# Start addresses of the standing weights, and 21 transposes whose result nobody reads

## The chip, the cores and the metric

The kernel runs on one core of a Trainium2 chip. The metric is the device time of one execution in microseconds (us); it is taken over several executions, and the median counts. A profile is one further execution, recorded instruction by instruction, with a time of its own.

## The reference

The reference is one layer of a decoder trunk for 256 tokens (SEQ) of width 2048 (D_MODEL), everything in float32:

```
h = rms_norm(x, norm1_g);  proj = h @ w_in              # 2048 x 6152: q, k, v of 8 + 8 heads, 8 gate columns
y_a = fox_attention(...);  y_b = dilated_attention(...)
x = x + concat(rms_norm(y_a, g_a), rms_norm(y_b, g_b)) @ w_out      # 2048 x 2048
h = rms_norm(x, norm2_g)
x = x + square(relu(h @ w_mlp_in)) @ w_mlp_out          # 2048 x 8192 and 8192 x 2048
return rms_norm(x, final_norm_g)
```

Nearly all the work lies in the four weight matrices, some 201 MB together, each of which is read once.

## The kernel before

**Three products for one.** A float32 product is made of three products in the fp32r type: a number is split into an upper part (what is left after it is rounded to fp32r) and a lower part (the rest), and upper x upper, upper x lower and lower x upper are summed in PSUM. The activations are split once and lie in `aT_hi`, `aT_lo` (input of a layer, features on the partitions) and in `yT_hi`, `yT_lo` (shown as `big_hi`, `big_lo` in the profile). The weights arrive in float32 in `raw` and are split as they come: ScalarE writes the upper part (`whi`, L180), VectorE the lower part (`wlo`, L181). One split covers 256 rows of a weight matrix by 512 columns; four buffers of `whi` and four of `wlo` are in turn.

**Chunks.** The program is a list of chunks of 512 weight columns. For each chunk 16 row blocks of 128 are multiplied (8 for half of w_out). There are two forms, and they matter here:

- *Weights moving* (chunks v, o and d: values, output projection, MLP down). The activations are loaded into the TensorE array as the standing operand, 128 columns wide, and 512 weight columns stream past (L314 to L316). A product is a load of 128 columns (PEld in the profile) and a MATMUL of 512 columns.
- *Weights standing* (chunks q, k and u, named in `TURNED`: queries, keys, MLP up). 128 weight columns are loaded, and the 256 tokens stream past (L331). The result comes out turned, features on the partitions, as the next stage wants it. For each of the four blocks of 128 weight columns three products follow each other: upper weights by `aT_hi`, the same upper weights by `aT_lo`, lower weights by `aT_hi`. There are 1536 of each of the three, 4608 in all: 1536 in the eight chunks q and k, in the first 310 us, and 3072 in the sixteen chunks u, in four stretches of 768 that alternate with the chunks d.

**Addresses.** All of this is about where in a partition an operand begins. A float32 element has 4 bytes. `whi` and `wlo` are tiles of 2*512 + 64 elements, 4352 bytes, which is 17 x 256 bytes; in the built program the first lies at byte 125952 = 492 x 256, so that all eight begin at a multiple of 256. A view into the tile skips the first `b` elements (L162 to L166):

```
            b = FAR if chunks[ci][0] in TURNED else NEAR
```

With `NEAR` = 8 a part begins 32 bytes behind a multiple of 256, with `FAR` = 56 it begins 224 bytes behind one. A block of 128 weight columns is 512 bytes, so all blocks begin at the same remainder. `aT_hi`, `aT_lo`, `big_hi` and `big_lo` lie 32 bytes behind a multiple of 256 (a small tile named `ahead`, L246, shifts them), and their rows of 256 tokens are 1024 bytes. So in the form "weights moving" both operands begin at 32, and in the form "weights standing" the moving operand begins at 32 and the load at 224.

**Transposes without a reader.** `settle` (L354) takes a PSUM tile and transposes the identity matrix into it three times. Nothing reads the tile. It runs at the end of each chunk v and at the end of each stretch of chunks d but the last: seven times, 21 transposes. Each of these places is where a stretch of weights moving ends and one of weights standing begins. There is one more such place, at the first chunk u, and there no `settle` stands.

**What sets the order.** The order is written out by hand. The main loop (L776 to L786) runs over the steps (256 weight rows each), issues the splits three steps ahead, and then the products of the step; side work (norms, attention, draining an accumulator) is hung on a product's number with `at` and is issued behind it by `run_side`. TensorE runs its instructions in this order; between two products of a chunk stand, now and then, the transposes and small products of the side work.

Of the kernel before, what the change touches and what calls it, by code (L numbers as in the profile page):

```python
# [11 lines left out]
F32 = mybir.dt.float32  # L12
# [7 lines left out]
P = 128  # L20
# [18 lines left out]
LEAD = 3  # L39


LINE, NEAR, FAR = 64, 8, 56
TURNED = "qku"
WARM, WARM2 = 8, 1

# [27 lines left out]
def kernel(  # L73
# [18 lines left out]
    nc = tc.nc  # L92
# [12 lines left out]
    psum = ctx.enter_context(tc.tile_pool(name="psum", bufs=2, space=PSUM))  # L105
# [4 lines left out]
    chunks = []  # L110
# [41 lines left out]
    def split(i, j0=0, n=2):  # L152
        if i >= len(steps):
            return
        if j0:
            return split_rows(i, j0, n)
        ci, s = steps[i]
        t = raws[ci, s // 2][:, 2 * (s % 2):2 * (s % 2) + 2, :]
        if ci == len(chunks) - 1 and s < 4:
            hi, lo = (a[:, 4 * s:4 * s + 4, :].rearrange("p (k j) s -> p k (j s)", k=2) for a in (aT_hi, aT_lo))  # L160
        else:
            b = FAR if chunks[ci][0] in TURNED else NEAR  # L162
            hi, lo = (
                wsplit.tile([P, 2 * CW + LINE], F32R, name=n)[:, b:b + 2 * CW].rearrange("p (j c) -> p j c", j=2)
                for n in ("whi", "wlo")
            )  # L166
        if chunks[ci][5] > CW:
            f = wsplit.tile([P, 2, 2 * NH], F32R, name="wf")
            fh, fl = f[:, :, :NH], f[:, :, NH:]
            nc.gpsimd.tensor_copy(fh, t[:, :, CW:])  # L170
            nc.gpsimd.tensor_tensor(fl, t[:, :, CW:], fh.bitcast(F32), op=ALU.subtract)
            forget_w[i] = f
        splits[i] = (hi, lo)
        split_rows(i, j0, n)

    def split_rows(i, j, n):
        ci, s = steps[i]
        hi, lo = (a[:, j:j + n, :] for a in splits[i])
        t = raws[ci, s // 2][:, 2 * (s % 2) + j:2 * (s % 2) + j + n, :CW]
        nc.scalar.activation(hi, t, AF.Copy)  # L180
        nc.vector.tensor_tensor(lo, t, hi.bitcast(F32), op=ALU.subtract)  # L181
# [4 lines left out]
    ident = one.tile([P, P], F32, name="ident")  # L186
# [148 lines left out]
    def products(i, j):  # L335
# [13 lines left out]
        if cols > CW:  # L349
            for n, part in enumerate(a[:2]):  # L350
                nc.tensor.matmul(accs["f"][:2 * NH, :SEQ], forget_w[i][:, j], part[:, kt, :],  # L351
                                 start=go and n == 0, stop=end and n == 1)

    def settle():  # L354

        p = psum.tile([P, 512], F32, name="tr")
        for n in range(3):
            nc.tensor.transpose(p[:, n * P:(n + 1) * P], ident, ident)  # L358


    side = {}
# [1 line left out]
    def at(i, f, *a):  # L363
        side.setdefault(i, []).append((f, a))
# [140 lines left out]
    probs, turned = {}, {}  # L505
# [171 lines left out]
    def last_chunk(done):  # L677

        ci = len(chunks) - 1
        what, key, _, _, _, _, kts = chunks[ci]  # L680
        i0 = len(steps) - kts // 2
        c0 = D_MODEL - CW
        for t, a, b, n in ((0, 0, CW, 3), (1, 0, CW // 2, 3), (1, CW // 2, CW, 4)):
            acc = psum.tile([P, CW], F32, name="acc", bufs=4)
            for kt in range(kts):
                if t == 0 and kt % 2 == 0:
                    split(done + 1 + kt // 2)
                product(acc[:, :b - a], operands(what, key), kt, t, splits[i0 + kt // 2], kt % 2, slice(a, b),
                        kt == 0, kt == kts - 1)
                if t == 0:  # L690
                    run_side(2 * i0 + kt)
            if b == CW:
                sum_before(t, n)
            add_down(acc, t, slice(c0 + a, c0 + b), n)
            if b == CW:
                finish(t, n, slice(c0 + a, c0 + b))
# [6 lines left out]
    for ci, (what, key, *_rest) in enumerate(chunks[:-1]):  # L703
        e = last_slot[what, key]
        if what == "v":
            at(e, drain_v, key, ci)
            at(e, settle)
            if key == 0:
                at(e, drain_f)
                at(e + 2, forget_gates)  # L710
                at(e + 6, gate_sums)
                at(e + 4, rel_row)
                at(e + 5, rel_back)
                at(e + 55, rel_turn)
        elif what in "qk":
            for half in range(2):
                late = half if what == "k" else (2 if key else 5) + 5 * half
                at(e + late, drain_qk, key, what, ci, half)
            if what == "k":
                kind = groups[key][4]  # L720
                for h in range(4):
                    n = e + 6 + 7 * (h // 2)
                    if kind == 0:
                        at(n - 3, decay_of, groups[key][3] * 4 + h)
                    at(n, scores, key, h)
                for h in range(4):
                    at(e + 20 + 7 * (h // 2), values, key, h)
                for h in range(4):
                    at(e + 13 + 7 * (h // 2), turn_probs, key, h)
                if key % 2:  # L730
                    at(e + 29, group_norm, kind)
        elif what == "o":
            at(e, drain_o, *key, ci)
            if key[0] == 1:
                at(e + 2, to_features, 4 * key[1], 16)
                at(e + 3, to_features, 4 * key[1] + 2, 16)
                if key[1] == 3:
                    at(e + 4, second_norm)
        elif what == "u":
            at(e, drain_u, key[1], ci)  # L740
        else:
            at(e, drain_d, *key, ci)
            if key[1] == 3:
                at(e, settle)
            if key == (ROUNDS - 1, 0):
                at(e - 8, load_gf)

    idle_products(WARM)
    split(0, 0, 1)
    gains(0, 16)  # L750
    to_features(0, 0, 1)
    split(0, 1, 1)
    to_features(1, 0, 1)
    idle_products(WARM2)
# [62 lines left out]
```

## Time and profile before

| | us |
|---|---|
| median of 3 timed executions | 1125.04 (1124.77 to 1125.28) |
| the profiled execution | 1123.52 |
| its span, from the first to the last instruction | 1121.7 |
| TensorE busy with products (PE) in the span | 1110.5 |
| TensorE busy with loads of the standing operand (PEld) | 1014.0 |
| VectorE, ScalarE, GpSimd busy | 643.0, 517.0, 33.3 |
| granted TensorE clock, mean | 0.998 |

The profile's page has a row for each group of instructions: its line, engine and operation, out<-in by the names of the tiles, the shapes, xcount, then the busy time in us and the mean time of one in ns, then the idle time of the engine before them. Products overlap in time: a MATMUL's own duration (280 ns) is longer than the distance to the next one. So what a product costs is read from the distance between starts, or from the length of a stretch divided by the number of products in it (the view of stretches, whose rows are: stretch from:to, its length, busy time of the engines and in brackets the number of instructions, granted clock, DMA share, GB/s).

### The profile page before, as it was taken

What the parts mean: (1) busy time and instruction counts of PE and PEld (TensorE: products, weight loads), DVE (VectorE), ACT (ScalarE), POOL (GpSimd) and SP (SyncE); (2) the same over time, 40 slices, a digit from 0 to 9 for tenths busy, and PEclk for the clock granted to TensorE, in tenths of its full rate; (3) what the DMA queues carried; (4) which work ended last, traced back from release to release, by engine and by line L of the source; (5) the groups of instructions that cost most, each with busy time, mean ns of one, the idle gap of its engine ahead of it and who ended that gap; (6) DMA issues with size and microseconds to landing.
All of it is one profiled execution on the core that took longest, in us unless ns stands there. A gap on an engine that the chain in (4) does not pass through costs nothing.

```text
span 1121.7 us, 17508 instructions
## 1 busy us (share of the span) xinstructions
PE 1110.5 (99%) x7362; PEld 1014.0 (90%) x7362; DVE 643.0 (57%) x805; ACT 517.0 (46%) x669; POOL 33.3 (3%) x58
## 2 busy tenths in 40 slices
PE   9999999999999999999999999999999999999996
PEld 7899899999988899998889998889998889999886
DVE  6666756656476675565545555555555554555564
ACT  6445545445454554553434454344444433454451
POOL 1100200000001000000000000000000000000000
PEclk9999999999999999999999999999999999999999
DMA  8665454545554556556565655565655566646641
GB/s 314 226 200 176 150 188 151 176 163 167 177 182 153 185 158 219 188 184 206 199 199 180 197 188 196 197 196 162 199 195 196 198 190 188 188 152 225 225 150 75
DMA packets 105098, 209.16 MB, mean 186 GB/s; under 512 B 3683, under 2 KB 4796, under 8 KB 104892
## 3 DMA queue, kind: packets, MB, share of 16 engines
q1 hardware_dynamic: 103868, 205.94, 55.4%
q0 software_dynamic: 304, 1.06, 0.4%
q8 instruction: 57, 0.93, 0.3%
q10 hardware_dynamic: 848, 1.06, 0.3%
q14 instruction: 21, 0.17, 0.0%
HBM read 205.93 MB, written 2.11 MB: 185 GB/s over the span
## 4 chain that ended last, share of the span: by engine, by line
PE 99%; DMA 0%; DVE 0%; POOL 0%; ACT 0%; DVEq 0%; issue 0%; ACTq 0%
PE acc L331 48%; PE acc L314 16%; PE acc L315 16%; PE acc L316 16%; PE sc L521 1%; PE sc L566 1%; PE tr L267 1%; PE tr L548 0%; DMA xs<-in_x_dram 0%; PE sc L351 0%; PE tr L358 0%; PE sc L518 0%; DVE xs L674 0%; PE sc L440 0%; PE tr L583 0%; POOL rstd L664 0%
## 5 line engine op out<-in xcount | busy, mean ns | idle before, releaser
L181 DVE TENSOR_TENSOR wlo<-raw,whi 128x1024 fp32r<-128x1024 f32 (+1 forms) x382 | 463.5, 1223 | 363.5 <-ACT whi L180 361.2
L180 ACT ACTIVATE whi<-raw 128x1024 fp32r<-128x1024 f32 (+1 forms) x382 | 399.5, 1053 | 406.9 <-PE acc L331 198.3
L331 PE MATMUL acc<-aT_hi,whi 128*128 128x256 f32 x1536 | 430.2, 280 | 0.1
L331 PE MATMUL acc<-aT_lo,whi 128*128 128x256 f32 x1536 | 427.0, 278 | 0.1
L331 PE MATMUL acc<-aT_hi,wlo 128*128 128x256 f32 x1536 | 426.6, 278 | 0.0
L331 PEld LDWEIGHTS acc<-aT_hi,whi 128*128 128x128 f32 x1536 | 288.3, 188 | 1.2 <-issue 0.6
L331 PEld LDWEIGHTS acc<-aT_hi,wlo 128*128 128x128 f32 x1536 | 288.3, 188 | 0.0
L331 PEld LDWEIGHTS acc<-aT_lo,whi 128*128 128x128 f32 x1536 | 287.9, 187 | 0.4 <-DVE aT_lo L257 0.3
L314 PE MATMUL acc<-whi,big_hi 128*128 128x512 f32 (+1 forms) x632 | 245.1, 388 | 0.0
L316 PE MATMUL acc<-wlo,big_hi 128*128 128x512 f32 (+1 forms) x632 | 244.4, 387 | 0.0
L315 PE MATMUL acc<-whi,big_lo 128*128 128x512 f32 (+1 forms) x632 | 244.3, 386 | 0.0
L316 PEld LDWEIGHTS acc<-wlo,big_hi 128*128 128x128 f32 x632 | 118.7, 188 | 24.2
L314 PEld LDWEIGHTS acc<-whi,big_hi 128*128 128x128 f32 x632 | 118.7, 188 | 23.7
L315 PEld LDWEIGHTS acc<-whi,big_lo 128*128 128x128 f32 x632 | 118.7, 188 | 23.4
L314 PE MATMUL acc<-whi,aT_hi 128*128 128x512 f32 x128 | 50.8, 397 | 0.0
L316 PE MATMUL acc<-wlo,aT_hi 128*128 128x512 f32 x128 | 50.1, 391 | 0.0
L315 PE MATMUL acc<-whi,aT_lo 128*128 128x512 f32 x128 | 50.0, 391 | 0.0
L254 DVE TENSOR_TENSOR big_lo<-nat,big_hi 128x512 fp32r<-128x512 f32 x32 | 22.2, 693 | 22.4 <-ACT big_hi L253 22.4
L253 ACT ACTIVATE big_hi<-nat 128x512 fp32r<-128x512 f32 x32 | 20.3, 634 | 26.1 <-DVE nat L615 26.1
L638 DVE SCALAR_TENSOR_TENSOR xs<-acc,rstd2sq,xs 128x512 f32<-128x512 f32 (+1 forms) x33 | 23.4, 734 | 10.6 <-PE acc L316 10.6
L316 PEld LDWEIGHTS acc<-wlo,aT_hi 128*128 128x128 f32 x128 | 24.0, 188 | 5.3
L314 PEld LDWEIGHTS acc<-whi,aT_hi 128*128 128x128 f32 x128 | 24.1, 188 | 4.5
(161 smaller groups left out, 516.0 us busy)
## 6 DMA issues: line engine op xcount, KB each, us to landing
raw<-in_w_mlp_in_dram SPq DMA_DIRECT2D x64, 1024.0 KB, 5.3
raw<-in_w_mlp_out_dram SPq DMA_DIRECT2D x64, 1024.0 KB, 5.1
raw<-in_w_in_dram SPq DMA_DIRECT2D x42, 1024.0 KB, 5.1
raw<-in_w_out_dram SPq DMA_DIRECT2D x16, 1024.0 KB, 5.0
raw<-in_w_in_dram SPq DMA_DIRECT2D x4, 1040.0 KB, 8.3
raw<-in_w_in_dram SPq DMA_DIRECT2D x4, 256.0 KB, 4.8
raw<-in_w_in_dram SPq DMA_DIRECT2D x2, 512.0 KB, 6.3
xs<-in_x_dram SPq DMA_DIRECT2D x2, 512.0 KB, 9.0
```

What stands on the lines that cost most here:

```text
L180: nc.scalar.activation(hi, t, AF.Copy)
L181: nc.vector.tensor_tensor(lo, t, hi.bitcast(F32), op=ALU.subtract)
L253: nc.scalar.activation(hi, src, AF.Copy)
L254: nc.vector.tensor_tensor(lo, src, hi.bitcast(F32), op=ALU.subtract)
L267: nc.tensor.transpose(p[:, j * SEQ + t * P:j * SEQ + (t + 1) * P], xs[:, t, c:c + P], ident)
L314: nc.tensor.matmul(acc, xh, hi[:, j, cols], start=go, stop=False)
L315: nc.tensor.matmul(acc, xl, hi[:, j, cols], start=False, stop=False)
L316: nc.tensor.matmul(acc, xh, lo[:, j, cols], start=False, stop=end)
L331: nc.tensor.matmul(acc, w[:, j, b * P:(b + 1) * P], a[:, kt, :], start=kt == 0 and b % 2 == 0 and n == 0, stop=kt == kts - 1 and n == 2, s ...
L521: nc.tensor.matmul(s[:, c0:c1], q[:, h, t * P:(t + 1) * P], k[:, h, :c1 - c0], start=n == 0 and kind == 1, stop=n == 2,)
L566: nc.tensor.matmul(y[:, o0:SEQ], v[:, t, h * P:(h + 1) * P], p[:, c0:c1], start=t == 0 and n == 0, stop=t == 1 and n == 2,)
L638: nc.vector.scalar_tensor_tensor(xs[:, t, cs], acc[:, :cs.stop - cs.start], rstd2sq[:, t:t + 1], xs[:, t, cs], op0=ALU.mult, op1=ALU.add)
```

## The change

Two things are done. The view into the tile gets a start of its own for the upper and for the lower part: in the chunks with standing weights the upper part begins at element 24, byte 96, and the lower part stays at element 56, byte 224. And `settle` is taken out with its calls. The tiles keep their size, and nothing else is written in another way.

```
-LINE, NEAR, FAR = 64, 8, 56
+LINE, NEAR, HIGH, LOW = 64, 8, 24, 56
 ...
         else:
-            b = FAR if chunks[ci][0] in TURNED else NEAR
+            turned = chunks[ci][0] in TURNED
             hi, lo = (
                 wsplit.tile([P, 2 * CW + LINE], F32R, name=n)[:, b:b + 2 * CW].rearrange("p (j c) -> p j c", j=2)
-                for n in ("whi", "wlo")
+                for n, b in (("whi", HIGH if turned else NEAR), ("wlo", LOW if turned else NEAR))
             )
 ...
-    def settle():
-
-        p = psum.tile([P, 512], F32, name="tr")
-        for n in range(3):
-            nc.tensor.transpose(p[:, n * P:(n + 1) * P], ident, ident)
 ...
         if what == "v":
             at(e, drain_v, key, ci)
-            at(e, settle)
 ...
             at(e, drain_d, *key, ci)
-            if key[1] == 3:
-                at(e, settle)
```

On TensorE the order of all other instructions stays. This is the place where the last stretch of chunks d that is followed by chunks u ends (934 us in the profile), before the change; `acc` is the accumulator in PSUM, `tr` the tile that `settle` takes:

```order
L316 MATMUL acc<-wlo,big_hi 128x512
L314 MATMUL acc<-whi,big_hi 128x512
L315 MATMUL acc<-whi,big_lo 128x512
L316 MATMUL acc<-wlo,big_hi 128x512
L358 MATMUL tr<-ident 128x128 x3
L331 MATMUL acc<-aT_hi,whi 128x256
L331 MATMUL acc<-aT_lo,whi 128x256
L331 MATMUL acc<-aT_hi,wlo 128x256
```

The same place in the changed program:

```order
L316 MATMUL acc<-wlo,big_hi 128x512
L314 MATMUL acc<-whi,big_hi 128x512
L315 MATMUL acc<-whi,big_lo 128x512
L316 MATMUL acc<-wlo,big_hi 128x512
L331 MATMUL acc<-aT_hi,whi 128x256
L331 MATMUL acc<-aT_lo,whi 128x256
L331 MATMUL acc<-aT_hi,wlo 128x256
```

The first product with standing weights now follows directly on the last one with moving weights. At the other six places the three transposes fall away in the same way; at the first of them (60 us) two small products for the gate columns stand ahead of them.

## The prediction, made before the changed kernel was run

> **What bounds the kernel now.** I read the page first, then the waits of TensorE, then stretches of products of one kind.
>
> ```profile
> span 1121.7 us, 17508 instructions
> PE 1110.5 (99%) x7362; PEld 1014.0 (90%) x7362; DVE 643.0 (57%) x805; ACT 517.0 (46%) x669; POOL 33.3 (3%) x58
> PE acc L331 48%; PE acc L314 16%; PE acc L315 16%; PE acc L316 16%; PE sc L521 1%; PE sc L566 1%; PE tr L267 1%; PE tr L548 0%; DMA xs<-in_x_dram 0%; PE sc L351 0%; PE tr L358 0%; PE sc L518 0%; DVE xs L674 0%; PE sc L440 0%; PE tr L583 0%; POOL rstd L664 0%
> ```
>
> The chain that ended last is TensorE from end to end: 48% of it are the products with standing weights (L331), 48% those with moving weights (L314 to L316). TensorE hardly waits; its waits are two at the start:
>
> ```profile
> PE sc L236 <- DVE relx L213: 1.2, 1, 1.2
> PE tr L267 <- DMA xs<-in_x_dram: 1.0, 1, 1.0
> ```
>
> So the time is the sum of the distances between products, and the question is what sets a distance. The view of stretches, for L331 alone, has a surprise. The first four rows are the long unbroken pieces of the q and k chunks, the last four the four stretches of u chunks (columns: length; busy PE and PEld, each with its count; clock; DMA share; GB/s):
>
> ```profile
> 70.58:93.24 22.66, 22.66 (x192) 22.61 (x192) 1.00 0.70 233
> 137.19:168.37 31.18, 31.18 (x264) 31.13 (x264) 1.00 0.59 196
> 212.69:243.87 31.18, 31.18 (x264) 31.14 (x264) 1.00 0.54 176
> 286.94:309.64 22.70, 22.70 (x192) 22.66 (x192) 1.00 0.56 182
> 411.92:494.97 83.05, 83.05 (x732) 83.01 (x732) 1.00 0.61 196
> 582.28:669.41 87.13, 87.13 (x768) 87.09 (x768) 1.00 0.60 193
> 756.72:847.26 90.54, 90.54 (x768) 90.50 (x768) 1.00 0.58 187
> 934.59:1025.13 90.54, 90.54 (x768) 90.50 (x768) 1.00 0.58 187
> ```
>
> The same 768 products take 87.13 us once and 90.54 us twice. Divided by their counts, rows five and six give 113.5 ns a product, the last two 117.9, the early four (107.72 us for 912) 118.1. There are two paces, and a stretch keeps the one with which it began. The clock is 1.00 in both, the DMA share nearly the same, and the addresses are the same; so what differs is a small shift in time with which a stretch starts, and which stays. With 256 moving columns a load of 128 weight columns and a product have nearly equal length (PEld is as busy as PE in these rows), so load and product run side by side all the time, reading the same memory.
>
> Two more places show other distances between the two addresses. In the last chunk there are products of 256 columns where both operands begin at 32, and in a stretch with moving weights products of 512 columns, both at 32 too:
>
> ```profile
> 1101.34:1112.73 11.39, 11.39 (x96) 1.00 0.24 92
> 494.97:582.03 87.06, 87.06 (x386) 1.00 0.59 193
> ```
>
> The first is 11.39 us for 95 to 96 starts, 119 to 120 ns; the second 226.7 ns for each of 384 (the count holds two neighbours). At distance 0 a product of 256 columns is dearer than at 192 in either pace; 3 x 113.5 = 340.5, 3 x 117.9 = 353.7 and 3 x 120 = 360: the slow pace lies as if two of three products paid the price of distance 0, some 6.6 ns more, and the third did not.
>
> **The change, part by part.** *The transposes.* The timeline shows TensorE passing from moving to standing weights, once without `settle` and once with it (columns: start, time, instruction):
>
> ```profile
> 406.71 0.39 PE L316 MATMUL acc<-wlo,big_hi 128*128 128x512 f32 x1
> 406.93 0.28 PE L331 MATMUL acc<-aT_hi,whi 128*128 128x256 f32 x1
> 407.05 0.28 PE L331 MATMUL acc<-aT_lo,whi 128*128 128x256 f32 x1
> ...
> 581.81 0.39 PE L316 MATMUL acc<-wlo,big_hi 128*128 128x512 f32 x1
> 582.03 0.49 PE L358 MATMUL tr<-ident 128*128 128x128 f32 x3
> 582.28 0.36 PE L331 MATMUL acc<-aT_hi,whi 128*128 128x256 f32 x1
> 582.48 0.28 PE L331 MATMUL acc<-aT_lo,whi 128*128 128x256 f32 x1
> ```
>
> From the last moving product to the second standing one it is 0.34 us without and 0.67 us with them. They lie on the path, nothing hides them: 0.33 us, seven times, **-2.3 us**. Nobody reads their tile and TensorE waits for none, so nothing else moves by this.
>
> *The address of the upper part.* ScalarE now writes `whi` 128 bytes lower, VectorE and TensorE read it there. ScalarE's and VectorE's splits, in a stretch where both begin at 224 and in one where both begin at 32:
>
> ```profile
> L180 ACT ACTIVATE whi<-raw 128x1024 fp32r<-128x1024 f32 x26 | 27.2, 1058 | 28.5 <-PE acc L331 28.5
> L180 ACT ACTIVATE whi<-raw 128x1024 fp32r<-128x1024 f32 x29 | 30.8, 1061 | 44.8 <-PE acc L315 44.7
> L181 DVE TENSOR_TENSOR wlo<-raw,whi 128x1024 fp32r<-128x1024 f32 x27 | 32.5, 1224 | 27.3 <-ACT whi L180 27.3
> L181 DVE TENSOR_TENSOR wlo<-raw,whi 128x1024 fp32r<-128x1024 f32 x30 | 36.6, 1226 | 36.2 <-ACT whi L180 35.9
> ```
>
> 1058 against 1061 ns and 1224 against 1226: the start does not matter to them. The sum of 1.06 + 1.22 us for 24 products is under the 2.72 us that these take at 113.5 ns, and ScalarE and VectorE work at the same time on different steps, so 0 us; were this cover gone, each would need over 2.7 us a step.
>
> *The loads.* 3072 of the 4608 loads now begin 64 bytes ahead of the moving operand's remainder (96 against 32), 1536 stay 64 behind it (224). No row of this kernel shows a load at +64, so its price is bounded. Above: 120 ns, the price at distance 0. Below: a load of 128 columns must fit, and transposes, whose load has the same 128 columns, show how close loads can follow:
>
> ```profile
> L358 PE MATMUL tr<-ident x21: 270/272/273, 60.0 to 934.6; 128*128 128x128 f32 x21
> ```
>
> Three of them take 0.49 us from the first start to the last end (above); less 0.272 for one and halved, 0.109 us. Between 109 and 120 I take 113.5: +64 is as far from 0 as -64 is, so it is nearest to the rows at 224, and of their two paces I take the fast one. The reason, which is an argument and no row: a slow stretch repeats the same meeting of load and product for hundreds of products, because all three loads of a triple begin at one remainder. With remainders 96, 96, 224 the distance changes twice in each triple, and a meeting that costs time in one product doesn't return in the next. Against it: with two distances there are also two chances to meet.
>
> All of L331 at 113.5 ns: the last two stretches give 2 x (90.54 - 87.13) = 6.8 us. The early 912 products give 107.72 - 912 x 0.1135 = 4.2 us. The other 624 products of q and k run in short pieces; at the same rate they would give 2.9 us, I take 2 since some pieces may be fast already. Together **-13.0 us**.
>
> Sum against the profiled execution: 1123.52 - 2.3 - 13.0 = 1108.2 us. The median of the runs shown is 1.5 above this execution, so I forecast **1109.7 us**, 1.4% less.
>
> A rule of the Trainium skill speaks against the change: in "SBUF — State Buffer", section "Who interferes with whom", TensorE has two read ports, one for the moving operand and one for the load, which are independent, and only a pair shared by VectorE and GpSimd makes engines wait. By it no start address can cost anything, and the result would be that of the first rival below. The trace agrees only in part: 113.5 and 117.9 ns at the same addresses mean that something between load and product does cost time, but no run here yet shows that the address is what decides.
>
> **The rivals.** *Only the transposes count (0.24).* The pace of a stretch is drawn when it starts and addresses don't matter. For it: two paces at equal addresses. Against it: 120 ns at distance 0. Then fast and slow stretches stay about as mixed, 1125.0 - 2.3 = 1122.7 us; with another draw, 1113 to 1128.
>
> *Without the transposes every stretch starts slow (0.16).* They shift the start in time, and may be what made a stretch fast. The one entry without them (406.93) goes on at 0.12 us a product. Against it: of seven entries with them only that at 582.28 was fast. Price: 1500 products of rows five and six at 117.9 instead of 113.5 ns, +6.6 us, less 2.3: 1125.0 + 4.3 = 1129.3 us. It decides if addresses are of no use and the start alone is.
>
> *The new distance is as bad as 0 (0.11).* If upper loads at +64 meet the moving reads as those at distance 0 do, 3072 products cost 120 ns. Against their present mean, (3 x 117.9 + 113.5 x 1.5)/4.5 = 116.4 by the share of fast products, 1500 of 4608, that is 3.6 x 3072 = +11 us, less 2.3: 1133.7 us.
>
> *Load and product no longer meet (0.07).* Then the load alone sets the distance, 109 ns: 4608 x 4.5 = 21 us below the forecast, 1089 us. For it only the transposes speak.
>
> In the Trainium skill, "TensorE: Matmul & The Clock Gate", section "Back-to-back issue gap", the gap is N/2.4 + 2.5 ns, 109.2 ns for 256 columns; by this the last rival would be right. No row of L331 here comes down to it.
>
> **How the numbers follow.** The forecast, all or nearly all of L331 fast, has 0.42. Its own range is 1106 to 1114 (an eighth of the products may stay slow, and the short pieces are an estimate). For 8 in 10 the range must take in the first two rivals and leaves out most of the last two: 1106 to 1130. A median of this kernel can be told from no change at about 0.2%, 2.25 us. Faster: 0.42 + 0.07, and 0.15 of the first rival, whose middle lies at the bound, 0.64. Within 0.2%: 0.07 of it and 0.04 of the others, 0.11. Slower: the rest, 0.25.
>
> **What would show it.** Right: in the view of stretches, 768 products of L331 take 87.1 us in all four u stretches and the early pieces run at 113.5 ns; the stretches of moving weights stay at 87.06 us; no row for L358. The first rival: again some stretches at 90.5. The second: all four at 90.5. The third: intervals of 120 ns ahead of or behind the upper loads, 92 us or more a stretch. Wrong in another way would be: stretches with moving weights that change, or TensorE waiting for ScalarE or VectorE.

## The result and the profile after

The changed kernel takes 1110.29 us (median of 4 executions, 1109.8 to 1111.35) against 1124.93 us before; the ratio is 0.9871 with a 95% interval of 0.9854 to 0.9888. That is 14.6 us or 1.3% less. Forecast were 1109.7 us, in a range of 1106 to 1130.

From the page of the changed kernel, the span, the busy times and the lines of the chain that ended last:

```profile
span 1108.3 us, 17466 instructions
...
PE 1096.8 (99%) x7341; PEld 1000.7 (90%) x7341; DVE 642.0 (58%) x805; ACT 517.3 (47%) x669; POOL 32.8 (3%) x58
...
PE acc L331 47%; PE acc L314 16%; PE acc L316 16%; PE acc L315 16%; PE sc L515 1%; PE sc L560 1%; PE tr L267 1%; DMA xs<-in_x_dram 0%; PE tr L542 0%; PE sc L351 0%; PE sc L512 0%; DVE xs L668 0%; PE sc L434 0%; PE tr L577 0%; POOL rstd L658 0%; PE tr L472 0%
```

TensorE is still the whole chain. It has 21 products and 21 loads fewer, the transposes. The view of stretches for L331, in the same eight places as before (length; busy PE and PEld with counts; clock; DMA share; GB/s):

```profile
71.16:93.03 21.87, 21.87 (x192) 21.83 (x192) 1.00 0.74 242
136.26:166.21 29.95, 29.95 (x264) 29.90 (x263) 1.00 0.63 207
209.94:239.88 29.94, 29.94 (x264) 29.90 (x263) 1.00 0.57 187
282.23:304.01 21.78, 21.78 (x192) 21.74 (x191) 1.00 0.57 188
406.24:489.30 83.06, 83.06 (x732) 83.02 (x732) 1.00 0.60 197
576.36:663.42 87.06, 87.06 (x768) 87.02 (x767) 1.00 0.60 194
750.49:837.55 87.06, 87.06 (x768) 87.02 (x767) 1.00 0.60 194
924.62:1011.68 87.06, 87.06 (x768) 87.02 (x767) 1.00 0.60 195
```

All u stretches have the fast pace now; the two that took 90.54 us take 87.06. The four early pieces take 103.54 us in place of 107.72. A stretch with moving weights is what it was (87.06 us before):

```profile
663.42:750.49 87.07, 87.07 (x387) 1.00 0.59 193
```

And this is an entry into a u stretch, without the transposes, in the timeline of the changed kernel:

```profile
750.26 0.39 PE L316 MATMUL acc<-wlo,big_hi 128*128 128x512 f32 x1
750.49 0.28 PE L331 MATMUL acc<-aT_hi,whi 128*128 128x256 f32 x1
750.61 0.28 PE L331 MATMUL acc<-aT_lo,whi 128*128 128x256 f32 x1
750.73 0.28 PE L331 MATMUL acc<-aT_hi,wlo 128*128 128x256 f32 x1
750.85 0.28 PE L331 MATMUL acc<-aT_hi,whi 128*128 128x256 f32 x1
750.96 0.28 PE L331 MATMUL acc<-aT_lo,whi 128*128 128x256 f32 x1
```

The first products stand 0.12 us apart, as in the one direct entry of before (at 406.93 us), which went on at that pace for its 24 products, until side work followed. Here the distance falls to 0.113 us within the first few products, and the row of the stretch shows that it stays there.

### The profile page after: what moved, and what is told of

Read it like the earlier page. It is cut to its first block, busy times and chain, and to the rows that moved or that the text cites. A ratio compares the mean times of both kernels' runs of the same rounds, so it can differ in the third digit from the quotient of the medians.

```text
span 1108.3 us, 17466 instructions
## 1 busy us (share of the span) xinstructions
PE 1096.8 (99%) x7341; PEld 1000.7 (90%) x7341; DVE 642.0 (58%) x805; ACT 517.3 (47%) x669; POOL 32.8 (3%) x58
## 4 chain that ended last, share of the span: by engine, by line
PE 99%; DMA 0%; DVE 0%; POOL 0%; DVEq 0%; ACTq 0%; issue 0%
PE acc L331 47%; PE acc L314 16%; PE acc L316 16%; PE acc L315 16%; PE sc L515 1%; PE sc L560 1%; PE tr L267 1%; DMA xs<-in_x_dram 0%; PE tr L542 0%; PE sc L351 0%; PE sc L512 0%; DVE xs L668 0%; PE sc L434 0%; PE tr L577 0%; POOL rstd L658 0%; PE tr L472 0%
## 5 line engine op out<-in xcount | busy, mean ns | idle before, releaser
L331 PE MATMUL acc<-aT_hi,whi 128*128 128x256 f32 x1536 | 426.7, 278 | 0.0
L331 PE MATMUL acc<-aT_lo,whi 128*128 128x256 f32 x1536 | 424.9, 277 | 0.0
L331 PE MATMUL acc<-aT_hi,wlo 128*128 128x256 f32 x1536 | 423.9, 276 | 0.0
L331 PEld LDWEIGHTS acc<-aT_hi,whi 128*128 128x128 f32 x1536 | 288.9, 188 | 1.4 <-ACT fu L398 0.6
L331 PEld LDWEIGHTS acc<-aT_lo,whi 128*128 128x128 f32 x1536 | 288.9, 188 | 0.5 <-DVE aT_lo L257 0.2
L331 PEld LDWEIGHTS acc<-aT_hi,wlo 128*128 128x128 f32 x1536 | 288.2, 188 | 0.0
L315 PEld LDWEIGHTS acc<-whi,big_lo 128*128 128x128 f32 x632 | 118.8, 188 | 23.5
```

The costliest lines, as they stand in the source:

```text
L315: nc.tensor.matmul(acc, xl, hi[:, j, cols], start=False, stop=False)
L331: nc.tensor.matmul(acc, w[:, j, b * P:(b + 1) * P], a[:, kt, :], start=kt == 0 and b % 2 == 0 and n == 0, stop=kt == kts - 1 and n == 2, s ...
```

## The experiments

Below, "distance" is the remainder of the load's start less that of the moving operand's start, in bytes modulo 256. In L331 the moving operand begins at 32 in every kernel, so there the distance is only another name for the load's own start; no kernel moves both, and whether the difference of the two counts or each start by itself is not shown. All kernels but the first have no transposes, as the changed one. The first two were executed 4 and 10 times, the others once; on the same chips the kernel before took 1123.4 to 1124.9 us. One execution shows the paces that its stretches took that once. That they come out alike again is likely, not shown: 13 executions of the kernel before lie within 2.8 us, less than the 3.4 us by which one u stretch differs between its paces.

### The two halves of the change

**Addresses alone.** The changed kernel with the transposes put back:

```
+    def settle():
+        p = psum.tile([P, 512], F32, name="tr")
+        for n in range(3):
+            nc.tensor.transpose(p[:, n * P:(n + 1) * P], ident, ident)
 ...
             at(e, drain_v, key, ci)
+            at(e, settle)
 ...
             at(e, drain_d, *key, ci)
+            if key[1] == 3:
+                at(e, settle)
```

> Upper parts at 96, lower at 224, the 21 transposes kept. Theory (the two different distances in each triple of products keep a stretch from locking into the slow pace, whatever the start): all four u stretches at 87.1 us for 768 products, 113.5 ns each, also the pieces of q and k; 1110.3 + 2.3 = 1112.6 us. Rival 1 (the removal of the transposes made the stretches start right, the addresses do nothing): paces mixed as in the kernel before, at least one u stretch at 90.5 us, 1118 to 1129 us. Rival 2 (distance +64 is a good one, alternation isn't needed): as the theory here.

It took 1112.39 us (4 executions, ratio to before 0.989, interval 0.9875 to 0.9905). The u stretches:

```profile
407.47:490.53 83.06, 83.06 (x732) 83.03 (x732) 1.00 0.61 196
577.85:665.00 87.15, 87.15 (x768) 87.12 (x768) 1.00 0.60 193
752.32:839.46 87.14, 87.14 (x768) 87.10 (x768) 1.00 0.60 193
926.77:1013.95 87.18, 87.17 (x768) 87.15 (x768) 1.00 0.60 194
```

All fast, whether the stretch starts behind transposes or not. The addresses alone give 12.5 of the 14.6 us. Rival 1, that the removal of the transposes did it, is out.

**Transposes alone.** Both parts at 224, as before, and no transposes:

```
-LINE, NEAR, HIGH, LOW = 64, 8, 24, 56
+LINE, NEAR, HIGH, LOW = 64, 8, 56, 56
```

> Upper and lower parts both at 224 as before, the 21 transposes removed. Theory: each stretch draws its pace by its start; entries without the transposes come directly behind a product with moving weights, and the only such entry before was slow, so most u stretches at 90.5 us; 1122 to 1129 us. Rival 1 (the removal did it): all four u stretches at 87.1 us, 1110.3 us. Rival 2: as the theory.

1125.97 us (10 executions), ratio to before 1.001, interval 1.0 to 1.0019. The u stretches:

```profile
410.75:493.80 83.05, 83.05 (x732) 83.02 (x732) 1.00 0.61 197
580.87:671.32 90.45, 90.45 (x768) 90.41 (x767) 1.00 0.59 188
758.37:848.82 90.45, 90.45 (x768) 90.40 (x767) 1.00 0.58 188
935.87:1026.32 90.45, 90.45 (x768) 90.40 (x767) 1.00 0.59 188
```

The three stretches that are entered directly are slow. The first, which starts behind four transposes of the side work, is fast as before. In the kernel before, one of these three, at 582 us, was fast with the transposes ahead of it: 90.45 - 87.13 = 3.3 us, against the 2.1 to 2.3 us that all 21 cost. Taken away by themselves they bring nothing.

### Which addresses

**One distance of +64.** Both parts at 96:

```
+LINE, NEAR, HIGH, LOW = 64, 8, 24, 24
```

> Upper and lower parts both at 96 (distance +64 in every product), no transposes. Theory (alternation counts): one distance again, so two paces possible again, and behind the direct entries the slow one is likelier: u stretches at 90.5 us, 1122 to 1129 us. Rival 2 (the distance +64 is good by itself): all four u stretches at 87.1 us, 1110.3 us. A third way: +64 in every product is as dear as distance 0, 92 us a stretch, 1135 us.

1122.49 us. One early piece and two of the u stretches:

```profile
210.05:241.15 31.10, 31.10 (x264) 31.05 (x263) 1.00 0.55 181
408.50:491.56 83.06, 83.06 (x732) 83.03 (x732) 1.00 0.61 197
578.63:669.08 90.45, 90.45 (x768) 90.41 (x767) 1.00 0.58 188
```

The same two paces as at 224, 113.5 and 117.8 ns. So +64 is no better than -64, and rival 2, that +64 is good by itself, is out: one distance, of either sign, is not enough.

**The pair the other way round.** Upper parts at 224, lower at 96:

```
+LINE, NEAR, HIGH, LOW = 64, 8, 56, 24
```

> Upper parts at 224, lower at 96, no transposes: the distances alternate as in the change, but only one load of three is at +64. Theory (alternation counts, not which part): all four u stretches at 87.1 us, 1110.3 us. Rival 2 (+64 is the good distance, and two of three loads need it): stretches slower than 87.1 us, by up to 3.4 us each, 1115 to 1127 us.

1117.02 us. The u stretches:

```profile
409.17:496.28 87.11, 87.11 (x732) 87.06 (x732) 1.00 0.58 189
583.37:670.42 87.05, 87.05 (x768) 87.01 (x767) 1.00 0.61 194
757.48:844.53 87.05, 87.05 (x768) 87.01 (x767) 1.00 0.60 195
931.60:1018.64 87.04, 87.04 (x768) 87.01 (x767) 1.00 0.60 194
```

The first row is 119.0 ns a product, the others 113.3. The theory, as it was put, falls here: the distance changes twice in each triple, and yet there is a slow pace, and a whole stretch keeps it. That an alternation as such prevents the slow pace is not so.

**Distance 0.** Both parts at 32:

```
+LINE, NEAR, HIGH, LOW = 64, 8, 8, 8
```

> Upper and lower parts both at 32, the distance 0 in every product with standing weights, no transposes. Theory (the distance between the load's and the moving operand's remainder sets the price, 0 being dear): every piece of L331 at 120 ns as in the last chunk, 92 us for 768, whatever the start; 4608 x 5.8 ns more than the change, 1137 us. Rival (any single distance gives the two paces 113.5 and 117.8 by the start alone): stretches at 87.1 or 90.5 us, 1118 to 1127 us.

1139.39 us.

```profile
415.41:503.33 87.92, 87.92 (x732) 87.88 (x732) 1.00 0.58 187
590.40:682.55 92.15, 92.15 (x768) 92.10 (x767) 1.00 0.58 185
769.62:861.77 92.15, 92.15 (x768) 92.10 (x767) 1.00 0.57 185
948.84:1040.99 92.15, 92.15 (x768) 92.10 (x767) 1.00 0.58 185
```

120.0 to 120.1 ns a product in every stretch, whatever its start: the price of the last chunk's products of 256 columns, now for all of L331. In the second row 766 of the 768 distances between starts are 120 ns in the trace, though ScalarE and VectorE are busy in only 44% and 52% of that time. So it is not their reads and writes of the split weights that slow the products down.

**The pair, moved by 64 bytes.** Upper parts at 32, lower at 160 (the same jump of 128 between them):

```
+LINE, NEAR, HIGH, LOW = 64, 8, 8, 40
```

> Upper parts at 32, lower at 160: the same order and the same jump of 128 bytes as in the change, the whole moved down by 64 bytes; distances 0, 0 and 128. Theory (the distance sets the price): two of three products pay 120 ns, the third 113.5 to 120, so 90.5 to 92 us a stretch from every start; 1128 to 1137 us. Rival (only the jump between upper and lower parts counts, the distance doesn't): all four u stretches at 87.1 us, 1110.3 us.

1135.44 us; 768 products take 91.47 us, 119.1 ns. The jump alone is worth nothing:

```profile
588.52:679.99 91.47, 91.47 (x768) 91.42 (x767) 1.00 0.58 186
```

**One distance of 128, and the pair moved by 32 bytes down and up.** Three kernels:

```
+LINE, NEAR, HIGH, LOW = 64, 8, 40, 40
+LINE, NEAR, HIGH, LOW = 64, 8, 16, 48
+LINE, NEAR, HIGH, LOW = 64, 8, 32, 64
```

> Upper and lower parts both at 160, distance 128 in every product with standing weights, no transposes. If what counts is the distance modulo 128 (so far 64 and 192 gave the same two paces): as distance 0, 120 ns in every piece, 92.15 us for 768, 1139 us. If it counts modulo 256 and 0 alone is dear, as far from it as one can be: 113.5 ns or less, 1110 us or below. In between, some 118 ns (with upper parts at 0 and lower at 128 a triple gave 119.1): 1128 us.

> Upper parts at 64, lower at 192: the change moved down by 32 bytes, distances 32 and 160. If the price goes by whole steps of 64 bytes, with 32 rounded to one side or the other: either 113.4 ns as the change (87.1 us a stretch, 1110.3 us) or 119.1 as with 32 and 160 (91.5 us, 1135 us). If it goes smoothly with the distance: in between, 116 ns, 89 us a stretch, 1123 us.

> Upper parts at 128, lower at 256, which is 0 of the next line: the change moved up by 32 bytes, distances 96 and 224. By whole steps: 113.4 ns (87.1 us, 1110.3 us) or 119.1 (1135 us), and the other way round than with 64 and 192 if 32 is rounded to one side; smoothly: 116 ns, 1123 us. A pace below 113.3 ns would make a version that beats the change.

(In the first of these expectations, "upper parts at 0 and lower at 128" means distances: it is the kernel with 32 and 160.) They took 1137.81, 1134.4 and 1128.55 us. One u stretch of each, in this order:

```profile
588.74:680.91 92.17, 92.17 (x768) 92.11 (x767) 1.00 0.58 185
```

```profile
587.95:679.25 91.30, 91.30 (x768) 91.25 (x767) 1.00 0.58 187
```

```profile
584.67:675.12 90.45, 90.45 (x768) 90.41 (x767) 1.00 0.59 188
```

128 alone is as dear as 0 (120.0 ns; its first u stretch ran at 118.8). Moved down by 32 bytes the pair costs 118.9 ns, moved up 117.8. Both are near the dear end, so it neither goes smoothly between 113.4 and 119.1, nor is one of the two moves the same as the change. All in one table, the distances in the order of the triple:

| upper, lower at | distances | ns a product, u stretches | one execution, us |
|---|---|---|---|
| 96, 224 (the change) | 64, 64, 192 | 113.4 to 113.5 in all four | 1110.29 (median) |
| 224, 96 | 192, 192, 64 | 119.0 once, 113.3 three times | 1117.02 |
| 96, 96 | 64, 64, 64 | 113.5 once, 117.8 three times | 1122.49 |
| 224, 224 | 192, 192, 192 | 113.5 once, 117.8 three times | 1125.97 (median) |
| 128, 0 | 96, 96, 224 | 117.8 to 117.9 | 1128.55 |
| 64, 192 | 32, 32, 160 | 118.5 to 118.9 | 1134.4 |
| 32, 160 | 0, 0, 128 | 119.1 to 119.2 | 1135.44 |
| 160, 160 | 128, 128, 128 | 118.8 once, 120.0 three times | 1137.81 |
| 32, 32 | 0, 0, 0 | 120.0 to 120.1 in all | 1139.39 |

### The form with moving weights

If distance 0 is dear for 256 columns, it might be so for 512, where load and moving operand both begin at 32. Three kernels, each the change with other starts for the moving weights:

```
-                for n, b in (("whi", HIGH if turned else NEAR), ("wlo", LOW if turned else NEAR))
+                for n, b in (("whi", HIGH if turned else 56), ("wlo", LOW if turned else 56))
```

and with 24 and 56, and with 40 and 40, in place of 56 and 56.

> The change, and in the chunks v, o and d the moving weights begin at 224 instead of 32, while the standing activations stay at 32: distance 64 in place of 0 for the products of 512 columns. Theory (distance 0 is dear): a product of 512 columns saves what one of 256 columns saves between distance 0 and 64, 6.6 ns, so 220 ns, 84.5 us for 384; 2256 x 6.6 = 15 us less, 1095 us, if the paces are the better one. Rival (226.7 is twice 113.4: the pace of the moving operand alone, in which the load has no part): 87.07 us a stretch as now, 1110.3 us.

> The change, and in the chunks v, o and d the moving upper weights begin at 96 and the moving lower weights at 224, the standing activations at 32: distances of 64 to either side. Theory (distance 0 is dear): 220 ns a product of 512 columns, 84.5 us for 384, 1095 us. Rival (the moving operand's own pace): 87.07 us a stretch, 1110.3 us.

> The change, with moving weights in the chunks v, o and d at 160 instead of 32: distance 128 for the products of 512 columns. Distance 64 gave 233.3 ns there and 0 gives 226.7. If it goes modulo 128: 226.7 ns as now, 87.07 us for 384, 1110.3 us. If 0 alone is good for this form: 233 ns or more, 89.6 us, 1125 us. If 128 is better than 0: below 87 us, and the version would beat the change.

They took 1124.58, 1117.27 and 1120.93 us. A stretch of 384 products of 512 columns in each:

```profile
671.05:760.64 89.59, 89.59 (x386) 1.00 0.58 188
```

```profile
666.76:755.23 88.47, 88.47 (x386) 1.00 0.58 190
```

```profile
668.22:757.44 89.22, 89.22 (x386) 1.00 0.58 189
```

The 87.07 us of the change are the best of the four: 226.7 ns at distance 0, 233.3 at 64, 232.3 at 128 and 230.4 with both signs of 64. The theory that distance 0 is dear falls for this form: here 0 is the good one. The rival forecast that nothing changes, and falls too. Whether the load has a part in it stays open: it began at 32 in all four, and only the moving operand's start was changed. None of the three is faster than the change. Their u stretches have its addresses, 96 and 224, and all twelve ran at 113.4 to 113.5 ns.

## Why the prediction was right, and where its reason was not

*What bounds.* TensorE from end to end, before and after: right.

*The transposes, -2.3 us.* The change and the kernel with the transposes put back differ by 1112.39 - 1110.29 = 2.1 us. Right in the main.

*The products, -13.0 us.* The kernel with addresses alone gives 1124.94 - 1112.39 = 12.5 us. By its terms: the last two u stretches gave 2 x (90.54 - 87.06) = 7.0 for 6.8 forecast, the early pieces 107.72 - 103.54 = 4.2 for 4.2. Over all 4608 products the distances from start to start add up to 538.7 us in the trace of before and to 526.2 after, 12.5 less; the first twelve took 0.6 us more after the change (last section), so the others gave 13.2, and the short pieces, taken at 2, gave 2. With the transposes the profiled executions differ by 1123.52 - 1110.05 = 13.5 us and not by 15.3; most of the 1.8 between was lost at the start, as the last section shows. That the median is nevertheless within 0.6 us of the forecast is partly luck: the forecast added 1.5 us from the profiled execution to the median, and the result has 0.2.

*The price of a load at +64.* Taken was 113.5 ns because +64 is as far from 0 as -64. That comparison holds: both at 96 gives the same two paces as both at 224. The lower bound of 109 ns was not reached by any of the nine pairs (113.3 is the least), so the last rival, that load and product no longer meet, is out; the upper bound of 120 is exactly the price at distance 0. The formula that the prediction quotes from the Trainium skill, "TensorE: Matmul & The Clock Gate", section "Back-to-back issue gap", is given there for a product by itself; in a stream of loads and products both set the spacing by that section. So its 109.2 ns was no case for the last rival.

*Why the fast pace.* This is the step that failed, though the number came out; that it did is luck, since the same argument forecast 1110.3 us for the mirror image, which took 1117.02. It said that two distances keep a costly meeting from returning. With 224 and 96 the distances alternate as well, and one u stretch ran at 119.0 ns; with 32 and 160, 64 and 192, 128 and 0 they alternate by the same 128 bytes, and every u stretch is slow. What the runs show is narrower: of nine pairs, 96 and 224 is the only one with which every u stretch ran at 113.4 to 113.5 ns, in five kernels, from starts with and without transposes. Why this pair has no slow pace and its mirror image has one is open: a fast triple costs 340 ns, a slow one of a single distance 353, one of the mirror image 357, one at distance 0 360, and no run here shows what the extra time is.

*Two dear products and a cheap one.* The prediction read a slow triple that way, from its sum. The trace of before does not bear it out: in the stretch at 756.72 us, 766 of the 768 distances are 117, 118 or 119 ns, and none is 113 or 120. Every product pays some 4.4 ns. That load and product have nearly equal length is not shown either: in that trace a load takes 188 ns and a product 280, and since both start some 118 ns apart, loads overlap one another as products do, so that PEld and PE are equally busy.

*The rivals.* "Only the transposes count" and "without the transposes every stretch starts slow" are both out for the changed addresses, and the second is right for the old ones, but for the first u stretch: with 224 and 224 all three that are entered directly were slow. The rule of the Trainium skill in "SBUF — State Buffer", section "Who interferes with whom", by which the load's port and the moving operand's are independent, does not hold for this kernel as the prediction used it, that no start address can cost anything: nothing but a start address was changed between 1110.29 and 1139.39 us, or between 87.06 and 92.15 us for the same 768 products. The measurement decides; whether it is the ports where the time is lost, no run here shows. "The new distance is as bad as 0" named a real price (120.0 ns), but for the wrong distance.

## What to carry to other kernels

Where a load of 128 columns and a moving operand of 256 columns run side by side, look at the distance between starts of products in each stretch, not at their mean: two paces at equal work show that something locks in. Then the start addresses of both operands are worth a sweep, in pairs and in both orders, for each form of product by itself: what was best for 256 columns (starts 64 bytes to both sides) was 1.6% dearer than distance 0 for 512. An instruction that does nothing but move a stretch's start should be taken out for a trial once the addresses are right: here 21 of them cost 2.1 us.

## What the runs showed of the hardware that was not expected

The start address of an operand in a partition, at equal length and layout, decides between 113.4 and 120.0 ns for a product of 256 columns, and between 226.7 and 233.3 for one of 512, in both cases 6.6 ns. A shift by 32 bytes (64 and 192 in place of 96 and 224) costs 5.5 ns a product.

The first products of an execution ran at about half pace in one profile and not in the other. Before, then after the change, in the timeline:

```profile
7.77 0.28 PE L331 MATMUL acc<-aT_hi,whi 128*128 128x256 f32 x1
7.89 0.28 PE L331 MATMUL acc<-aT_lo,whi 128*128 128x256 f32 x1
```

```profile
8.93 0.41 PE L331 MATMUL acc<-aT_lo,whi 128*128 128x256 f32 x1
9.15 0.41 PE L331 MATMUL acc<-aT_hi,whi 128*128 128x256 f32 x1
```

0.12 us apart against 0.21. The first twelve products took 2.56 us after the change (7.82 to 10.38) and 1.92 before (7.03 to 8.95), 0.6 us more, and they began 0.8 us later. So the changed execution was 1.4 us behind when they were done, of the 1.8 that are missing against the forecast. It does not belong to the change: of the profiles of the fourteen kernels here ten have products 0.21 us apart at this place, among them kernels with the transposes and without, and four do not. The clock column shows 1.00 in the first 10 us of both executions and does not tell them apart. In the Trainium skill, "TensorE: Matmul & The Clock Gate", section "What's actually happening", the array's clock is halved until a free-running window of 3.4 us has been busy; 0.21 us for what takes 0.12 is a factor of 1.8, which is near that, but the clock record here doesn't confirm it.
